# A prefix log-sum-exp kernel: one table set for Exp and Ln, and tiles of 512 rows instead of 256

## The chip, the cores and the metric

The kernel runs on one core of a Trainium2 chip. The metric is the device time of one execution in microseconds (us), lower is better. The unchanged kernel ("before") takes 1329.4 us as the median of three runs (1328.58 to 1329.96).

In the profiles PE is TensorE, which does the matrix products here (PEld is its loading of weights), ACT is ScalarE (Exp and Ln), DVE is VectorE (the adds), POOL is GpSimd and SP is SyncE; ACTq and SPq are the queues from which ScalarE and SyncE issue DMA transfers. L58 is line 58 of the kernel's file.

## The reference

The input `x` and the output are f32 arrays of shape (8, 4096, 2048). Along the second axis, each output row is the running log of the sum of exponentials:

```
out[:, 0] = x[:, 0]
for t in 1 .. 4095:
    mx        = max(out[:, t-1], x[:, t])
    out[:, t] = mx + log(exp(out[:, t-1] - mx) + exp(x[:, t] - mx))
```

The kernels here compute it as a running sum of `exp(x)` (matrix products with triangular matrices of ones, summed in PSUM) followed by a log. Both arrays must move: 268 MB in and 268 MB out.

## The kernel before

Two batch elements `j` are worked on in turn, so there are always two independent running sums. A tile holds 256 rows of one batch element: partition `p` holds rows `2p` and `2p+1` side by side, 4096 columns.

```python
    xpool = ... bufs=4        # input tiles,  f32,  16 KiB per partition each
    epool = ... bufs=4        # exp(x), bf16,        8 KiB
    opool = ... bufs=4        # output tiles, f32,  16 KiB
    ppool = ... bufs=1, PSUM  # two running sums [128, 2048] f32
    for bp in range(0, B, PAIR):
        ...
        for k in range(NBLK):
            for j in range(PAIR):
                ...
                xt = xpool.tile([P, 2 * D], f32)
                nc.sync.dma_start(out=xt, in_=x_v[b, k])            # L58, load, queue of SyncE
                et = epool.tile([P, 2 * D], bf16)
                nc.scalar.activation(et, xt, ACT.Exp)               # L61
                ...   # matmuls with Li and Ls: sum up to row 2p     # L65, L69
                ot = opool.tile([P, 2 * D], f32)
                nc.scalar.activation(ot[:, :D], ps, ACT.Ln)         # L75, first Ln
                nc.vector.tensor_add(ot[:, D:], ps, et[:, D:])      # L76, adds row 2p+1
                nc.scalar.activation(ot[:, D:], ot[:, D:], ACT.Ln)  # L77, second Ln
                nc.scalar.dma_start(out=o_v[b, k], in_=ot)          # L79, store, queue of ScalarE
                if k < NBLK - 1:
                    ...   # matmuls with Ui and Us complete the sum  # L84, L88
```

The program text does not fix the order of instructions on each engine. The framework that builds the kernel picks an order for each engine at build time, so that for example the Exp of the next tile goes ahead of the second Ln of this one.

The softmax here doesn't subtract the row's maximum and nothing guards it: scores larger than these inputs give would overflow.

Of the kernel before, what the change touches and what calls it, by code (L numbers as in the profile page):

```python
# [1 line left out]

# [4 lines left out]


@with_exitstack
def kernel(  # L10
    ctx: ExitStack,
    tc: tile.TileContext,
    x: bass.AP,
    out: bass.AP,
):
    nc = tc.nc
    f32 = mybir.dt.float32
    bf16 = mybir.dt.bfloat16
    ACT = mybir.ActivationFunctionType

    B, S, D = x.shape
    P = 128
    SB = 256
    NBLK = S // SB
    FD = 512
    NC = D // FD
    PAIR = 2

    const = ctx.enter_context(tc.tile_pool(name="const", bufs=1))
    Li = const.tile([P, P], bf16)  # L30
    masks.make_upper_triangular(nc, Li, val=1.0, diag=True)
    Ls = const.tile([P, P], bf16)
    masks.make_upper_triangular(nc, Ls, val=1.0, diag=False)
    Ui = const.tile([P, P], bf16)
    masks.make_lower_triangular(nc, Ui, val=1.0, diag=False)
    Us = const.tile([P, P], bf16)
    masks.make_lower_triangular(nc, Us, val=1.0, diag=True)

    xpool = ctx.enter_context(tc.tile_pool(name="xpool", bufs=4))
    epool = ctx.enter_context(tc.tile_pool(name="epool", bufs=4))  # L40
    opool = ctx.enter_context(tc.tile_pool(name="opool", bufs=4))
    ppool = ctx.enter_context(tc.tile_pool(name="ppool", bufs=1, space=bass.MemoryType.PSUM))

    x_v = x.rearrange("b (k p two) d -> b k p (two d)", p=P, two=2)
    o_v = out.rearrange("b (k p two) d -> b k p (two d)", p=P, two=2)

    for bp in range(0, B, PAIR):
        psums = [
            ppool.tile([P, D], f32, name=f"ps_{bp}_{j}", tag=f"ps{j}")
            for j in range(PAIR)  # L50
        ]
        for k in range(NBLK):
            for j in range(PAIR):
                b = bp + j
                ps = psums[j]

                xt = xpool.tile([P, 2 * D], f32)
                nc.sync.dma_start(out=xt, in_=x_v[b, k])  # L58

                et = epool.tile([P, 2 * D], bf16)  # L60
                nc.scalar.activation(et, xt, ACT.Exp)  # L61

                for c in range(NC):
                    lo, hi = c * FD, (c + 1) * FD
                    nc.tensor.matmul(  # L65
                        ps[:, lo:hi], Li, et[:, lo:hi],
                        start=(k == 0), stop=False, skip_group_check=True,
                    )
                    nc.tensor.matmul(  # L69
                        ps[:, lo:hi], Ls, et[:, D + lo : D + hi],  # L70
                        start=False, stop=False, skip_group_check=True,
                    )

                ot = opool.tile([P, 2 * D], f32)
                nc.scalar.activation(ot[:, :D], ps, ACT.Ln)  # L75
                nc.vector.tensor_add(ot[:, D:], ps, et[:, D:])  # L76
                nc.scalar.activation(ot[:, D:], ot[:, D:], ACT.Ln)  # L77

                nc.scalar.dma_start(out=o_v[b, k], in_=ot)  # L79

                if k < NBLK - 1:
                    for c in range(NC):
                        lo, hi = c * FD, (c + 1) * FD
                        nc.tensor.matmul(  # L84
                            ps[:, lo:hi], Ui, et[:, lo:hi],
                            start=False, stop=False, skip_group_check=True,
                        )
                        nc.tensor.matmul(  # L88
                            ps[:, lo:hi], Us, et[:, D + lo : D + hi],
                            start=False, stop=False, skip_group_check=True,  # L90
                        )


# [1 line left out]
_INS = ['x']  # L95
_OUTS = [((8, 4096, 2048), 'float32')]


# [23 lines left out]
```

## Time and profile before

| | before |
|---|---|
| time, median | 1329.4 us |
| ScalarE busy | 1268.8 us, 96% |
| of it table loads | 326 us, 254 loads |
| load queue and store queue, share of the 16 DMA engines | 51.4% + 47.3% |

These are lines of the profile's page of before: busy time per engine; the DMA's busy tenths and its GB/s in 40 slices of the span; the two DMA queues (packets, MB, share of the 16 engines' time; q1 is the loads, q10 the stores); the chain of waits by engine; and groups of instructions (count, busy us, mean ns, then the idle time before them).

```profile
PE 654.6 (49%) x1945; PEld 244.5 (18%) x1984; DVE 289.3 (22%) x128; ACT 1268.8 (96%) x638; POOL 1.9 (0%) x12
...
DMA  9999999999999999999999999999999999999976
GB/s 397 424 414 408 413 414 411 413 412 412 411 409 410 404 400 414 409 413 411 414 412 410 409 417 399 414 397 412 413 412 409 414 407 414 410 411 410 408 326 277
...
q1 hardware_dynamic: 18432, 268.44, 51.4%
q10 hardware_dynamic: 18432, 268.44, 47.3%
...
ACT 83%; PE 10%; issue 4%; ACTq 1%; DMA 1%; DVE 0%; another core or an unknown queue 0%; SPq 0%
...
L61 ACT ACTIVATE et<-xt 128x4096 bf16<-128x4096 f32 x128 | 462.9, 3617 | 9.1 <-DMA xt<-in_x_dram 7.7
...
L61 ACT ACT_TABLE_LOAD x127 | 162.9, 1283 | 3.1 <-PEq L106 0.8
L77 ACT ACT_TABLE_LOAD x84 | 107.8, 1283 | 1.5
...
L75 ACT ACT_TABLE_LOAD x43 | 55.2, 1283 | 0.7
```

ScalarE is the busy one, and a quarter of its work is table loads of 1283 ns, because Exp and Ln come from different table sets and alternate. The DMA is also shown at 9 tenths throughout.

Two views of waits say which of the two holds the other back. The first is ScalarE's waits, the second those of the load queue (what waited, on what; us in total, times, longest).

```profile
ACT et L61 <- DMA xt<-in_x_dram: 7.7, 2, 6.4
```

```profile
SPq L58 <- ACT et L61: 1207.2, 124, 11.9
```

ScalarE waited 7.7 us for loads in the whole run. The loads waited 1207 us for ScalarE to free an input buffer. ScalarE sets the pace.

The next view is four windows of 3 us of before, after start, end and length the busy time of each engine. The last three numbers of each line are TensorE's granted clock, the DMA's busy share and its GB/s.

```profile
609.00:612.00 3.00, 3.00 (x12) 1.17 (x10) 0.00 (x0) 2.98 (x2) 0.00 (x0) 0.71 1.02 437
612.00:615.00 3.00, 1.38 (x7) 0.52 (x6) 0.00 (x0) 2.99 (x3) 0.00 (x0) 1.00 0.97 371
615.00:618.00 3.00, 0.00 (x0) 0.00 (x0) 0.00 (x0) 2.53 (x2) 0.00 (x0) 0.92 1.07 339
618.00:621.00 3.00, 0.19 (x1) 0.10 (x1) 2.29 (x1) 2.97 (x3) 0.00 (x0) 0.50 0.89 360
```

Most of the time the DMA moves 431 to 437 GB/s. Once per three tiles it dips for some 9 us while its "busy" share stays near 1. In this dip (612 to 621 us) loads take 79% of the DMA's time, as the stores have nearly run out, and their packets get longer: 754 ns on average. The packet records have 611 ns as the usual time of a 16 KiB packet in both queues; 32768 of them on 16 engines make 1251 us. That is an estimate of the DMA's floor for this kernel.

### The profile page before, as it was taken

The page shows a single profiled execution, that of the slowest core. Times are in us where ns is not written, and L with a number is a line of the kernel's source. Part 1 is how long each engine was busy: PE and PEld are TensorE (multiplying, and loading weights), DVE is VectorE, ACT ScalarE, POOL GpSimd, SP SyncE. Part 2 cuts the span into 40 slices and gives each one's busy share as a digit, 9 for nine tenths or more (in the row PEclk, how much of TensorE's full clock was granted, in tenths as well). Part 3 has the DMA queues.
Part 4 walks back from the last instruction along what each step waited for, and adds up shares of the span by engine and source line. Part 5 has one row for each costly group of instructions (what it writes and reads, how often), then busy time and mean ns, then how long its engine had stood idle before and what let it go on. Part 6 is the DMA issues. An engine that isn't in the chain of part 4 may idle for free.

```text
span 1326.9 us, 5421 instructions
## 1 busy us (share of the span) xinstructions
PE 654.6 (49%) x1945; PEld 244.5 (18%) x1984; DVE 289.3 (22%) x128; ACT 1268.8 (96%) x638; POOL 1.9 (0%) x12
## 2 busy tenths in 40 slices
PE   4455544544454445544454555444544455555442
PEld 1111211211121111211111221111211121122110
DVE  1222222222222222222222222222222222222222
ACT  7999999999999999999999999999999999999996
POOL 0000000000000000000000000000000000000000
PEclk9777777777777777777677777777777777777776
DMA  9999999999999999999999999999999999999976
GB/s 397 424 414 408 413 414 411 413 412 412 411 409 410 404 400 414 409 413 411 414 412 410 409 417 399 414 397 412 413 412 409 414 407 414 410 411 410 408 326 277
DMA packets 36890, 537.22 MB, mean 405 GB/s; under 512 B 4096, under 2 KB 4096, under 8 KB 4096
## 3 DMA queue, kind: packets, MB, share of 16 engines
q1 hardware_dynamic: 18432, 268.44, 51.4%
q10 hardware_dynamic: 18432, 268.44, 47.3%
q8 instruction: 15, 0.25, 0.1%
q14 instruction: 11, 0.09, 0.0%
HBM read 268.44 MB, written 268.44 MB: 405 GB/s over the span
## 4 chain that ended last, share of the span: by engine, by line
ACT 83%; PE 10%; issue 4%; ACTq 1%; DMA 1%; DVE 0%; another core or an unknown queue 0%; SPq 0%
ACT et L61 35%; ACT ot L77 18%; ACT ot L75 12%; ACT L61 9%; ACT L77 8%; PE ps L65 6%; PE ps L69 4%; ACTq L79 1%; DMA xt<-in_x_dram 1%; ACT L75 0%; DVE ot L76 0%; ACTq L75 0%; SPq L58 0%
## 5 line engine op out<-in xcount | busy, mean ns | idle before, releaser
L76 DVE TENSOR_TENSOR ot<-ps,et 128x2048 f32<-128x2048 f32 x128 | 289.3, 2288 | 1025.7 <-ACT ot L75 1025.7
L61 ACT ACTIVATE et<-xt 128x4096 bf16<-128x4096 f32 x128 | 462.9, 3617 | 9.1 <-DMA xt<-in_x_dram 7.7
L84 PE MATMUL ps<-et,Ui 128*128 128x512 bf16 x480 | 261.3, 544 | 387.7 <-DVE ot L76 385.2
L65 PE MATMUL ps<-et,Li 128*128 128x512 bf16 x512 | 245.3, 479 | 268.4 <-ACT et L61 266.3
L75 ACT ACTIVATE ot<-ps 128x2048 f32<-128x2048 f32 x128 | 240.3, 1877 | 32.4 <-ACT ot L77 19.7
L88 PE MATMUL ps<-et,Us 128*128 128x512 bf16 x463 | 254.3, 549 | 0.0
L77 ACT ACTIVATE ot<-ot 128x2048 f32<-128x2048 f32 x128 | 239.8, 1904 | 1.6 <-DVE ot L76 0.6
L69 PE MATMUL ps<-et,Ls 128*128 128x512 bf16 x490 | 224.6, 458 | 0.0
L61 ACT ACT_TABLE_LOAD x127 | 162.9, 1283 | 3.1 <-PEq L106 0.8
L88 PEld LDWEIGHTS <-Us 128*128 128x128 bf16 x480 | 61.5, 128 | 499.3 <-issue 485.2
L69 PEld LDWEIGHTS <-Ls 128*128 128x128 bf16 x512 | 59.8, 117 | 360.8 <-issue 328.1
L77 ACT ACT_TABLE_LOAD x84 | 107.8, 1283 | 1.5
L84 PEld LDWEIGHTS <-Ui 128*128 128x128 bf16 x480 | 63.4, 132 | 107.9 <-issue 93.5
L65 PEld LDWEIGHTS <-Li 128*128 128x128 bf16 x512 | 59.8, 117 | 97.6 <-issue 60.6
L75 ACT ACT_TABLE_LOAD x43 | 55.2, 1283 | 0.7
masks.py:102 POOL TENSOR_SCALAR_AFFINE_SELECT Ui<-Ui 128x128 bf16<-128x128 bf16 x1 | 0.3, 299 | 0.0
masks.py:102 POOL TENSOR_SCALAR_AFFINE_SELECT Us<-Us 128x128 bf16<-128x128 bf16 x1 | 0.3, 298 | 0.0
masks.py:66 POOL TENSOR_SCALAR_AFFINE_SELECT Ls<-Ls 128x128 bf16<-128x128 bf16 x1 | 0.3, 297 | 0.0
masks.py:66 POOL TENSOR_SCALAR_AFFINE_SELECT Li<-Li 128x128 bf16<-128x128 bf16 x1 | 0.3, 296 | 0.0
masks.py:101 POOL MEMSET Ui<- 128x128 bf16 x1 | 0.2, 208 | 0.0
masks.py:101 POOL MEMSET Us<- 128x128 bf16 x1 | 0.2, 208 | 0.0
masks.py:65 POOL MEMSET Ls<- 128x128 bf16 x1 | 0.2, 206 | 0.0
(5 smaller groups left out, 0.6 us busy)
## 6 DMA issues: line engine op xcount, KB each, us to landing
xt<-in_x_dram SPq DMA_DIRECT2D x128, 2048.0 KB, 13.6
out_dram<-ot ACTq DMA_DIRECT2D x128, 2048.0 KB, 17.3
```

Source lines behind the costliest of these rows:

```text
L61: nc.scalar.activation(et, xt, ACT.Exp)
L65: nc.tensor.matmul(ps[:, lo:hi], Li, et[:, lo:hi], start=(k == 0), stop=False, skip_group_check=True,)
L69: nc.tensor.matmul(ps[:, lo:hi], Ls, et[:, D + lo : D + hi], start=False, stop=False, skip_group_check=True,)
L75: nc.scalar.activation(ot[:, :D], ps, ACT.Ln)
L76: nc.vector.tensor_add(ot[:, D:], ps, et[:, D:])
L77: nc.scalar.activation(ot[:, D:], ot[:, D:], ACT.Ln)
L79: nc.scalar.dma_start(out=o_v[b, k], in_=ot)
L84: nc.tensor.matmul(ps[:, lo:hi], Ui, et[:, lo:hi], start=False, stop=False, skip_group_check=True,)
L88: nc.tensor.matmul(ps[:, lo:hi], Us, et[:, D + lo : D + hi], start=False, stop=False, skip_group_check=True,)
```

## The change

The intent: load one table set that has both Exp and Ln, so that ScalarE no longer reloads tables; and put four rows in a partition, so that each descriptor moves 32 KiB. Rows two to four are made by chained adds on VectorE. The tile doubles to 4 MB, and so the buffers go from 4/4/4 to 3/2/2 (input/bf16/output) to fit: 192 KiB per partition.

```diff
+    nc.scalar.preload_act_table_set("natural_log_exp_and_others")
-    SB = 256
-    NBLK = S // SB
+    R = 4
+    NBLK = S // (P * R)
...
-    xpool ... bufs=4    epool ... bufs=4    opool ... bufs=4
+    xpool ... bufs=3    epool ... bufs=2    opool ... bufs=2
...   (matmuls moved to a helper, the same number of them)
-                xt = xpool.tile([P, 2 * D], f32)
+                xt = xpool.tile([P, R * D], f32)
                 nc.sync.dma_start(out=xt, in_=x_v[b, k])
-                nc.scalar.activation(et, xt, ACT.Exp)
+                nc.scalar.activation(et[:, :half], xt[:, :half], ACT.Exp)      # L80
+                nc.scalar.activation(et[:, half:], xt[:, half:], ACT.Exp)      # L81
...
-                nc.vector.tensor_add(ot[:, D:], ps, et[:, D:])
+                nc.scalar.activation(ot[:, :D], ps, ACT.Ln)                     # L86
+                nc.vector.tensor_add(ot[:, D : 2 * D], ps, et[:, D : 2 * D])    # L87
+                for r in range(2, R):
+                    nc.vector.tensor_add(                                       # L89
+                        ot[:, r * D : (r + 1) * D],
+                        ot[:, (r - 1) * D : r * D],
+                        et[:, r * D : (r + 1) * D],
+                    )
                 nc.scalar.activation(ot[:, D:], ot[:, D:], ACT.Ln)              # L95
                 nc.scalar.dma_start(out=o_v[b, k], in_=ot)                      # L97
```

(The first Ln, L86, was there before too; it is shown for its line number.)

More of the change, by code (lines that the diff above doesn't have):

```diff
@@ L37, with accumulate @@
     masks.make_lower_triangular(nc, Us, val=1.0, diag=True)
-    xpool = ctx.enter_context(tc.tile_pool(name="xpool", bufs=4))
-    epool = ctx.enter_context(tc.tile_pool(name="epool", bufs=4))
-    opool = ctx.enter_context(tc.tile_pool(name="opool", bufs=4))
+    xpool = ctx.enter_context(tc.tile_pool(name="xpool", bufs=3))
+    epool = ctx.enter_context(tc.tile_pool(name="epool", bufs=2))
+    opool = ctx.enter_context(tc.tile_pool(name="opool", bufs=2))
     ppool = ctx.enter_context(tc.tile_pool(name="ppool", bufs=1, space=bass.MemoryType.PSUM))
-    x_v = x.rearrange("b (k p two) d -> b k p (two d)", p=P, two=2)
-    o_v = out.rearrange("b (k p two) d -> b k p (two d)", p=P, two=2)
+    x_v = x.rearrange("b (k p r) d -> b k p (r d)", p=P, r=R)
+    o_v = out.rearrange("b (k p r) d -> b k p (r d)", p=P, r=R)
+    def accumulate(ps, et, first, rest, start):
+        for r in range(R):
+            w = first if r == 0 else rest
+            for c in range(NC):
+                lo, hi = c * FD, (c + 1) * FD
+                nc.tensor.matmul(
+                    ps[:, lo:hi], w, et[:, r * D + lo : r * D + hi],
+                    start=(start and r == 0), stop=False, skip_group_check=True,
+                )
     for bp in range(0, B, PAIR):
@@ L55 @@
                 ps = psums[j]
-                xt = xpool.tile([P, 2 * D], f32)
+                xt = xpool.tile([P, R * D], f32)
                 nc.sync.dma_start(out=xt, in_=x_v[b, k])
-                et = epool.tile([P, 2 * D], bf16)
-                nc.scalar.activation(et, xt, ACT.Exp)
-                for c in range(NC):
-                    lo, hi = c * FD, (c + 1) * FD
-                    nc.tensor.matmul(
-                        ps[:, lo:hi], Li, et[:, lo:hi],
-                        start=(k == 0), stop=False, skip_group_check=True,
-                    )
-                    nc.tensor.matmul(
-                        ps[:, lo:hi], Ls, et[:, D + lo : D + hi],
-                        start=False, stop=False, skip_group_check=True,
-                    )
-                ot = opool.tile([P, 2 * D], f32)
-                nc.scalar.activation(ot[:, :D], ps, ACT.Ln)
-                nc.vector.tensor_add(ot[:, D:], ps, et[:, D:])
+                et = epool.tile([P, R * D], bf16)
+                half = R * D // 2
+                nc.scalar.activation(et[:, :half], xt[:, :half], ACT.Exp)
+                nc.scalar.activation(et[:, half:], xt[:, half:], ACT.Exp)
+                accumulate(ps, et, Li, Ls, k == 0)
+                ot = opool.tile([P, R * D], f32)
+                nc.scalar.activation(ot[:, :D], ps, ACT.Ln)
[5 more added lines that the diff above has]
+                        et[:, r * D : (r + 1) * D],
+                    )
                 nc.scalar.activation(ot[:, D:], ot[:, D:], ACT.Ln)
@@ L81 @@
                 if k < NBLK - 1:
-                    for c in range(NC):
-                        lo, hi = c * FD, (c + 1) * FD
-                        nc.tensor.matmul(
-                            ps[:, lo:hi], Ui, et[:, lo:hi],
-                            start=False, stop=False, skip_group_check=True,
-                        )
-                        nc.tensor.matmul(
-                            ps[:, lo:hi], Us, et[:, D + lo : D + hi],
-                            start=False, stop=False, skip_group_check=True,
-                        )
+                    accumulate(ps, et, Ui, Us, False)
 _INS = ['x']
```

## The prediction

> **What bounds it now.** ScalarE. The page's busy line has ACT at 1268.8 of 1326.9 us (96%); the waits view shows ScalarE waiting only 7.7 us for loads, while the load queue waits 1207 us for ScalarE to free its input buffers. The chain of waits is 83% ACT. Of ACT's time 326 us (162.9 + 107.8 + 55.2 in the groups, 254 loads of 1283 ns) is table loading, because Exp and Ln alternate. Without it ACT would need 943 us.
>
> But DMA stands right behind: the slices show 9 tenths and about 411 GB/s. Stretches of 3 us (600 to 693 us) read 431 to 437 GB/s mostly, with one dip per 30.7 us (three tiles) to about 340 to 390 GB/s over 9 us, when the stores have run out and a nearly empty load queue shows long packets. The page's queue lines give 0.473 x 1327 x 16 / 16384 = 613 ns per 16 KiB store packet, 666 ns per load packet; the packet records have 611 ns as the usual value for both. 32768 packets of 611 ns on 16 engines are 1251 us. I read the rest (about 55 us of lengthened load packets) as ScalarE not asking early enough, not as a DMA limit. The Trainium skill ("DMA: Bandwidth & Descriptors", "Where 436 GB/s comes from") puts the fabric ceiling at 435 GB/s; 431 to 437 agrees. So the change can win 5 to 6%, not the 25% of the table loads.
>
> **What the change does.**
> - Table loads: 254 to 1 or 2. The Trainium skill ("ScalarE: Activation LUTs", "Table sets") lists Exp and Ln in this set. Saves 325 us of ACT.
> - ACT per 512-row tile: two Exp of 3.62, Ln of 2048 at 1.88, Ln of 6144 at about 5.33 (estimate from the slope between the 1.90 and 3.62 us activations): 14.4 us, times 64 is 925 us, about 73%.
> - VectorE: 192 adds of about 2.29 us, 440 us (from 289), chained.
> - Matmuls: same number.
> - DMA: same bytes, half the packets. 4-byte packets take 9 ns; if that is the fixed part, a 32 KiB packet takes 1213 ns and the floor is 1242 us (estimate).
> - Buffers: 3/2/2 of double size. An output buffer's loop (Ln 1.9 + adds 6.9 + Ln 5.3 + about 2 + store 19.6 at half rate = 36 us) is under two tile periods (39 us): tight, but while stores are out, loads run at full rate.
>
> **Sum.** First packet after about 2.6 us; DMA 1242 to 1251; tail with DMA idle about 18 (last load: Exp 7.2, matmuls 3.4, Ln and adds 8.8, Ln 5.3, issue, then a 9.8 us store; one other store fills part); remaining dips about 5; the time sits 2.5 above the span. I say **1274 us, range 1258 to 1300**. Faster by over 2%: 0.87; within 2%: 0.11; slower: 0.02.
>
> **What the profile would show.** ACT at 70 to 75% with one table load; ScalarE waiting hundreds of us for loads; slices at 425 to 435 GB/s throughout; 8192 data packets per queue at 1213 to 1225 ns; DVE 440 us; the chain no longer mostly ACT.
>
> **What would make it wrong.** (1) The dips belong to the DMA, so it stays at 411 GB/s: near 1325. (2) Two output or two bf16 buffers make ScalarE wait for stores or matmuls while the input buffers stand full, so DMA idles each tile: 1300 or more. (3) Table loads stay; even 190 leave ACT at 1170, under DMA. (4) Ramp and tail grow with the doubled tile by more than 10 us.

## The result, and the profile after

The changed kernel takes 1396.7 us (median of four runs, 1396.3 to 1398.33), against 1329.7 us for before in the same comparison. The ratio is 1.051 (95% interval 1.049 to 1.052): 5% slower, where 4% faster was predicted. Ratios in this document are the mean time of one kernel's fast runs over that of the other's in the same rounds, so not quite the ratio of the medians that are quoted. Results are correct unless said otherwise.

The lines of the changed kernel's page that answer to those of before:

```profile
PE 579.5 (42%) x1882; PEld 220.5 (16%) x1920; DVE 434.1 (31%) x192; ACT 905.5 (65%) x257; POOL 1.9 (0%) x12
...
DMA  9989989899898989989899797997979989899865
GB/s 406 420 348 406 435 340 427 363 421 407 368 427 363 406 376 406 435 361 423 376 416 430 316 430 335 414 434 313 430 336 406 436 335 429 351 407 434 337 266 241
...
q10 hardware_dynamic: 9216, 268.44, 45.7%
q1 hardware_dynamic: 9216, 268.44, 45.5%
...
ACT 35%; DMA 28%; DVE 26%; issue 10%; ACTq 0%; PE 0%
...
L95 ACT ACTIVATE ot<-ot 128x6144 f32<-128x6144 f32 x64 | 338.9, 5318 | 308.2 <-DVE ot L89 308.2
...
L89 DVE TENSOR_TENSOR ot<-ot,et 128x2048 f32<-128x2048 f32 x128 | 288.9, 2288 | 2.2
...
L27 ACT ACT_TABLE_LOAD x1 | 1.3, 1283 | 0.8 <-PEq L115 0.8
```

What was predicted of the parts happened: one table load, ScalarE busy for 905 us (925 predicted), VectorE for 434 us, 8192 data packets in each queue. What was predicted of the whole did not: ScalarE does not wait hundreds of us for loads, and the slices do not stay at 425 to 435 GB/s. The DMA is no longer always busy. Its queues add up to 91.2% of the span instead of 98.7%, so packets fill all but 8.8% of 1394.6 us, about 123 us, and the slices, but for the last two, swing between 313 and 436 GB/s. The chain of waits is now split three ways, ScalarE 35%, DMA 28%, VectorE 26%: no engine is full, they wait for one another in turn.

ScalarE's waits of the changed kernel:

```profile
ACT ot L95 <- DVE ot L89: 308.2, 47, 9.1
ACT ot L86 <- DMA out_dram<-ot: 143.3, 15, 14.7
ACT et L80 <- DMA xt<-in_x_dram: 10.9, 1, 10.9
```

It hardly waits for loads (10.9 us). It waits 308 us for VectorE's adds (47 times) and 143 us for stores, 15 times, some 9.6 us each: the first Ln (L86) needs an output buffer that is still being stored. Busy 905.5, adds 308 and stores 143 make 1357 of the 1394.6 us.

Here is one such wait. First ScalarE, then VectorE, of the changed kernel in order of time (start, duration, engine, line, operation, tile; in brackets the idle time before it and what ended it).

```profile
660.59 3.60 ACT L81 ACTIVATE et<-xt 128x4096 bf16<-128x4096 f32 x1
664.09 1.85 ACT L86 ACTIVATE ot<-ps 128x2048 f32<-128x2048 f32 x1
673.38 1.88 ACT L86 ACTIVATE ot<-ps 128x2048 f32<-128x2048 f32 x1 [7.43 <-DMA out_dram<-ot]
684.21 10.54 ACT L95 ACTIVATE ot<-ot 128x6144 f32<-128x6144 f32 x2 [8.96 <-DVE ot L89]
689.57 5.55 ACTq L97 DMA_DIRECT2D out_dram<-ot  x2
```

```profile
665.98 2.29 DVE L87 TENSOR_TENSOR ot<-ps,et 128x2048 f32<-128x2048 f32 x1 [21.17 <-ACT ot L86]
675.29 2.29 DVE L87 TENSOR_TENSOR ot<-ps,et 128x2048 f32<-128x2048 f32 x1 [7.02 <-ACT ot L86]
677.49 8.89 DVE L89 TENSOR_TENSOR ot<-ot,et 128x2048 f32<-128x2048 f32 x4
```

Tile one gets its first Ln at 664.09 and its first add at 665.98. But the lists of both engines then name tile two: ScalarE's next instruction is tile two's first Ln, which waits until 673.38 for an output buffer; VectorE's next is tile two's first add, which waits for that Ln. Tile one's remaining adds stand behind it, in a row of four with tile two's, and its second Ln starts at 684.21. So tile one's 4 MB store is issued 25.5 us after its first Ln, although its own work is 1.9 + 6.9 + 5.3 = 14.1 us. In the two windows of 3 us before that issue the DMA runs dry (the last two numbers are its busy share and GB/s):

```profile
684.00:687.00 3.00, 0.00 (x0) 0.00 (x0) 2.38 (x2) 2.79 (x1) 0.00 (x0) 0.50 0.41 175
687.00:690.00 3.00, 0.00 (x0) 0.00 (x0) 0.00 (x0) 3.00 (x2) 0.00 (x0) 0.50 0.00 0
```

The three input buffers are full, and no store is there yet.

The Trainium skill ("PSUM — Partial Sum Buffer", section "Engine vs sequencer instructions") says that the queues of ScalarE and VectorE are strict FIFO. The two timelines agree: nothing passes the waiting instruction, although tile one's second add could have started some 9 us earlier, at the end of its first (668.27).

### The profile page after: what moved, and what is told of

The parts are those of the page before. It is cut to its first block, busy times and chain, and to the rows that moved or that the text cites. A ratio compares the mean times of both kernels' runs of the same rounds, so it can differ in the third digit from the quotient of the medians.

```text
span 1394.6 us, 4663 instructions
## 1 busy us (share of the span) xinstructions
PE 579.5 (42%) x1882; PEld 220.5 (16%) x1920; DVE 434.1 (31%) x192; ACT 905.5 (65%) x257; POOL 1.9 (0%) x12
## 4 chain that ended last, share of the span: by engine, by line
ACT 35%; DMA 28%; DVE 26%; issue 10%; ACTq 0%; PE 0%
DMA out_dram<-ot 27%; ACT ot L95 20%; DVE ot L89 18%; DVE ot L87 8%; ACT ot L86 6%; ACT et L80 6%; ACT et L81 3%; DMA xt<-in_x_dram 1%; PE ps L60 0%; ACTq L97 0%; ACTq L86 0%; ACTq L80 0%
## 5 line engine op out<-in xcount | busy, mean ns | idle before, releaser
L95 ACT ACTIVATE ot<-ot 128x6144 f32<-128x6144 f32 x64 | 338.9, 5318 | 308.2 <-DVE ot L89 308.2
L87 DVE TENSOR_TENSOR ot<-ps,et 128x2048 f32<-128x2048 f32 x64 | 146.6, 2292 | 933.4 <-ACT ot L86 933.4
L89 DVE TENSOR_TENSOR ot<-ot,et 128x2048 f32<-128x2048 f32 x128 | 288.9, 2288 | 2.2
L60 PE MATMUL ps<-et,Li 128*128 128x512 bf16 x251 | 91.3, 499 | 468.0 <-ACT et L80 467.7
L80 ACT ACTIVATE et<-xt 128x4096 bf16<-128x4096 f32 x64 | 230.6, 3604 | 18.1 <-DMA xt<-in_x_dram 10.9
L81 ACT ACTIVATE et<-xt 128x4096 bf16<-128x4096 f32 x64 | 230.4, 3601 | 0.0
L86 ACT ACTIVATE ot<-ps 128x2048 f32<-128x2048 f32 x64 | 119.1, 1861 | 145.6 <-DMA out_dram<-ot 143.3
L60 PE MATMUL ps<-et,Us 128*128 128x512 bf16 x658 | 204.2, 471 | 1.5 <-issue 1.1
L60 PE MATMUL ps<-et,Ui 128*128 128x512 bf16 x220 | 83.7, 517 | 278.5 <-DVE ot L87 278.0
L60 PEld LDWEIGHTS <-Ls 128*128 128x128 bf16 x768 | 86.3, 112 | 166.1 <-issue 108.9
L60 PEld LDWEIGHTS <-Li 128*128 128x128 bf16 x256 | 28.3, 111 | 517.5 <-issue 493.0
L60 PEld LDWEIGHTS <-Ui 128*128 128x128 bf16 x224 | 25.1, 112 | 323.0 <-issue 310.3
L27 ACT ACT_TABLE_LOAD x1 | 1.3, 1283 | 0.8 <-PEq L115 0.8
```

The lines of the kernel that those rows point to most:

```text
L27: nc.scalar.preload_act_table_set("natural_log_exp_and_others")
L60: nc.tensor.matmul(ps[:, lo:hi], w, et[:, r * D + lo : r * D + hi], start=(start and r == 0), stop=False, skip_group_check=True,)
L80: nc.scalar.activation(et[:, :half], xt[:, :half], ACT.Exp)
L81: nc.scalar.activation(et[:, half:], xt[:, half:], ACT.Exp)
L87: nc.vector.tensor_add(ot[:, D : 2 * D], ps, et[:, D : 2 * D])
L89: nc.vector.tensor_add(ot[:, r * D : (r + 1) * D], ot[:, (r - 1) * D : r * D], et[:, r * D : (r + 1) * D],)
```

## The experiments

Eighteen more kernels ran. The table has ScalarE's account for those that the argument rests on, all from the busy lines and the waits views, in us. "Adds" is the second Ln waiting for VectorE, "stores" the first Ln waiting for an output buffer, "matmuls" the first Ln waiting for PE. 3/2/2 and the like are numbers of input, bf16 and output buffers; "8 columns" and "64 columns" are the changed kernel with a needless Exp of so many columns, which changes the order (see below). Times are medians; the waits are those of the one profiled run.

| kernel | time | busy | adds | stores | loads | matmuls |
|---|---|---|---|---|---|---|
| before | 1329 | 1269 | 1 | 0 | 8 | 11 |
| changed | 1397 | 906 | 308 | 143 | 11 | 2 |
| 256 rows, combined tables | 1260 | 916 | 1 | 289 | 8 | 31 |
| 256 rows, 3/2/2 | 1353 | 921 | 10 | 198 | 8 | 219 |
| 256 rows, 3/2/4 | 1314 | 921 | 11 | 0 | 8 | 354 |
| changed, with table loads | 1358 | 1034 | 270 | 15 | 11 | 1 |
| changed, 2/2/3 | 1294 | 907 | 309 | 0 | 43 | 10 |
| changed, later loads | 1322 | 906 | 308 | 69 | 11 | 2 |
| changed, Ln per row | 1418 | 923 | 166 | 297 | 11 | 2 |
| 8 columns | 1311 | 914 | 153 | 194 | 13 | 2 |
| 64 columns | 1290 | 917 | 336 | 0 | 14 | 0 |

### The combined table set alone

```diff
     ACT = mybir.ActivationFunctionType
+    nc.scalar.preload_act_table_set("natural_log_exp_and_others")     # in the kernel before
```

> The kernel before with the combined table set alone (256-row tiles, 4/4/4 buffers). Theory (the DMA limit of the prediction was right, and the slowdown comes from the 512-row tile with few buffers): the loads of tables go from 254 to 1, DMA stays supplied, about 1272 to 1285 us, 430 GB/s in the slices. Rival (the 411 GB/s of before was already the limit of mixed loads and stores): 1315 to 1330 us, with ACT idle.

Measured: 1259.5 us (1259.0 to 1259.64), ratio 0.948 (0.946 to 0.949). This is the fastest correct kernel, 5% faster than before, and below even the theory's range. Lines of its page:

```profile
PE 648.3 (52%) x1984; PEld 238.8 (19%) x1984; DVE 293.1 (23%) x128; ACT 916.2 (73%) x385; POOL 1.9 (0%) x12
...
DMA  9999999999999999999999999999999999999997
GB/s 385 431 432 430 431 431 431 430 431 431 429 431 431 431 429 432 431 431 431 431 432 430 430 432 431 429 432 431 431 430 430 432 429 433 430 431 430 431 431 325
...
q1 hardware_dynamic: 18432, 268.44, 50.0%
q10 hardware_dynamic: 18432, 268.44, 49.9%
```

The DMA runs at 429 to 433 GB/s in every slice between the first and the last, and its queues take 99.9% of the span. So the dips of before were ScalarE's doing, and the DMA floor of the prediction (1251 us) was right. Summed over both queues and shared over 16 engines, the packets' excess over 611 ns fell from about 56 us to under 3. ScalarE's 289 us of waits for stores cost nothing here: both queues always hold work, and the wait is for the DMA, which is the limit.

This splits the change in two: the table set is worth -70 us, so the 512-row tile with its buffers costs +137 us on top of it. (The two parts are not independent, as the run with table loads below shows.)

### 256 rows with as few buffers

```diff
-    xpool bufs=4, epool bufs=4, opool bufs=4      # combined tables, 256 rows
+    xpool bufs=3, epool bufs=2, opool bufs=2
```

> The kernel before with the combined table set and 3 input, 2 bf16 and 2 output buffers, as the changed kernel has, but of half the size. Theory (the number of output buffers alone starves the DMA, whatever the tile size): 1360 us or more, with ScalarE waiting for stores and fully idle DMA in every tile. Rival (it is the longer serial chain of the four-row tile, Ln, three adds, Ln, before a 4 MB store): below 1310 us.

Measured: 1353.2 us (1346.6 to 1365.2), ratio 1.016 (1.011 to 1.021). Neither number was hit by the median, but the rival is out: with half-size tiles fewer buffers eat the gain of the tables, and more. (With fewer buffers the build also chose another order on ScalarE than with 4/4/4, so the count and the order that came with it are not separated.) Two waits appear in the profiled run, the slowest of the four at 1365 us: 198 us for stores and 219 us for matmuls, so it is not output buffers only.

```diff
+    xpool bufs=3, epool bufs=2, opool bufs=4      # the order on ScalarE's list is the same as with 3/2/2
```

> 256-row tiles, combined tables, 3 input, 2 bf16 and 4 output buffers; its ScalarE order is the same as that of the run with 3/2/2 (1353 us). Theory (output buffers are what starves it): 1265 to 1290 us, no waits for stores to speak of. Rival (two bf16 buffers or three input buffers cost as much; 219 us of waits for matmuls point there): 1310 us or more.

Measured: 1314.4 us (1314.0 to 1314.9), ratio 0.989 (0.987 to 0.990), outside the theory's range and in the rival's. Two more output buffers took the 198 us of waits for stores away and brought 39 us; waits for matmuls grew to 354 us. In this build ScalarE runs first Ln, Exp, second Ln of one tile at a time, and each first Ln waits some 3 us for matmuls. Which of the other two pools causes that was not tried. So at 256 rows theory and rival each explain a part: output buffers cost about 39 us, and the other 55 us (1314 against 1260) come with the other two pools and the order that the build chose for them.

### The changed kernel with table loads

```diff
-    nc.scalar.preload_act_table_set("natural_log_exp_and_others")
```

> The changed kernel without the combined table set, so table loads return. Theory (in the changed kernel the chain Ln, adds, Ln, store, buffer is the limit and ScalarE is on it part of the time): table loads of 1.28 us that fall on the chain lengthen it, 1400 to 1480 us. Rival (ScalarE has 35% of slack, so table loads vanish in it): within 1% of 1397 us.

Measured: 1358.4 us (two runs, 1357.0 and 1359.7), ratio 1.022 (1.020 to 1.024). Both expectations missed: with 128 us more work for ScalarE the changed kernel is 38 us faster. Leaving the table loads aside, the lists of ScalarE and VectorE are the same instruction for instruction, so this is not another order. ScalarE's waits for stores fell from 143 to 15 us. So the table set, worth 70 us with 256 rows, costs 38 us here, and with table loads in both kernels the 512-row tile costs only 29 us (1358 against 1329). A possible reason: the table loads delay the Exp, so the input buffers come free later and the next loads start later. The next run tests that.

### Loads that start later

```diff
+    hold = const.tile([P, 1], f32)
...
                 nc.scalar.activation(ot[:, :D], ps, ACT.Ln)
+                nc.gpsimd.tensor_add(hold, xt[:, :1], ot[:, :1])   # keeps xt until here
```

> The changed kernel, where GpSimd reads one column of the input tile after the first Ln of that tile, so that an input buffer comes free (and the next 4 MB load starts) some 5 to 15 us later; ScalarE's order is unchanged. Found so far: the four-row kernel with table loads (same order on ScalarE) takes 1358 us, without them 1397 us. Theory (a faster ScalarE frees input buffers earlier, and the loads then share the DMA with the stores that the output buffers wait for): later loads make the stores land sooner, ScalarE's 143 us of waits for stores shrink, the time falls to 1350 to 1385 us. Rival (fewer loads in flight only leave DMA more idle; the table loads helped for another reason): 1400 us or more.

Measured: 1322.4 us (1321.1 to 1326.8), ratio 0.995 (0.993 to 0.997): 74 us faster than the changed kernel, for one needless instruction on GpSimd per tile. It is better than the theory's range. ScalarE's waits (L97 is the second Ln here, L87 the first):

```profile
ACT ot L97 <- DVE ot L91: 308.1, 47, 9.0
ACT ot L87 <- DMA out_dram<-ot: 68.8, 15, 9.3
```

Waits for adds are the same 308 us; waits for stores fell by 74.5 us, which is the whole gain. Loads and stores run on the same 16 DMA engines. The Trainium skill ("DMA: Bandwidth & Descriptors", "Issuing engines are not separate DMA queues") says that DMAs interleave there whichever engine issued them, and the packet records of the changed kernel agree: while both queues have work, loads take 52% of the engines and stores 48%. In the changed kernel an input buffer comes free early, its load takes half of the DMA from a store that ScalarE is waiting for, and then the loads run out of buffers and the DMA idles. Starting the load later lets the store go first. The traces bear this out: the 15 stores that ScalarE waited for took 25.2 us on average from issue to its next Ln in the changed kernel, with loads on 42% of the DMA meanwhile; here they took 20.2 us, with loads on 33%. And the queues now fill 97.3% of the span (48.9 + 48.4) instead of 91.2%, so the time in which the DMA is free fell from 123 to 36 us.

### One buffer moved from input to output

```diff
-    xpool bufs=3, epool bufs=2, opool bufs=2
+    xpool bufs=2, epool bufs=2, opool bufs=3
```

> The changed kernel with one 32 KiB buffer moved from the input pool to the output pool (2/2/3 instead of 3/2/2). The order of the instructions on ScalarE is nearly the same. Theory (two output buffers are the cause): ScalarE's 143 us of waits for stores go and the time falls to about 1320 to 1360 us, though loads have less room. Rival (any loss of room for loads costs as much, the total of buffers is what matters): 1390 us or more.

Measured: 1293.7 us (1290.4 to 1294.8), ratio 0.973 (0.971 to 0.975): 103 us faster than the changed kernel with the same memory, again better than the range. ScalarE's list is the same, so the comparison is clean. Its waits:

```profile
ACT ot L95 <- DVE ot L89: 309.2, 47, 9.1
ACT et L80 <- DMA xt<-in_x_dram: 43.3, 12, 11.0
```

No wait for stores is left; 32 us more are spent waiting for loads.

### The output tile in halves, and a Ln for each row

The first of these stores each half of the output tile by itself, from two pools of half tiles, after its own Ln.

```diff
-                ot = opool.tile([P, R * D], f32)
+                oa = opool.tile([P, 2 * D], f32, tag="oa")    # rows one and two
+                ob = opool.tile([P, 2 * D], f32, tag="ob")    # rows three and four
...
+                nc.scalar.activation(oa[:, D:], oa[:, D:], ACT.Ln)
+                nc.scalar.dma_start(out=o_v[b, k][:, : 2 * D], in_=oa)
+                nc.scalar.activation(ob, ob, ACT.Ln)
+                nc.scalar.dma_start(out=o_v[b, k][:, 2 * D :], in_=ob)
```

> The changed kernel with each output tile in two halves of 16 KiB per partition (2 buffers each, the same memory), each with its own Ln and its own 2 MB store, the first half stored while rows three and four are still to be done. Theory (two whole output tiles, each held from the first Ln to the landing of a 4 MB store, are the bottleneck): halves come free sooner and the DMA has a store to move earlier, 1270 to 1330 us. Rival (total bytes of output buffer count, not their grain): 1380 us or more.

Measured: 1296.9 us (1291.3 to 1302.8), ratio 0.975 (0.971 to 0.979), as the theory said: 100 us faster in the same memory. Waits for stores are 11 us. The build's order changed here as well, but not to fewer pairs in which both first Ln come in a row: there are 24 of 32 (16 in the changed kernel). How much of the gain is the halves and how much the order is not separated.

```diff
-                nc.scalar.activation(ot[:, D:], ot[:, D:], ACT.Ln)
+                for r in range(1, R):
+                    nc.scalar.activation(ot[:, r*D:(r+1)*D], ot[:, r*D:(r+1)*D], ACT.Ln)
```

> The changed kernel with the Ln over 6144 columns cut into three of 2048, so that a row's Ln runs beside the add of the next row; one 4 MB store as before. Theory (the serial chain Ln, three adds, Ln of 5.3 us, store holds the output buffer): some 3.5 us shorter per tile where nothing else waits, up to 64 x 3.5 / 2 = 110 us in all, so 1290 to 1370 us. Rival (only the store's time matters): within 1% of 1397 us.

Measured: 1417.7 us (1416.4 and 1418.9), ratio 1.066 (1.064 to 1.068). A miss: slower, though the wait for adds halved to 166 us. The build's order had changed too. Both tiles' first Ln now come ahead of any second Ln in every pair (in the changed kernel, in every second pair), with five single-row Ln ahead of the first store. Waits for stores doubled: 297 us, 31 times. This pointed to the order.

The two ideas that worked, together: halves of the output tile with 2 input and 3 + 3 half output buffers.

> 512-row tiles, combined tables, output tiles in halves, 2 input, 2 bf16 and 3 + 3 half output buffers. Theory (output space was the limit, input space is then next): 1265 to 1295 us, ScalarE waiting for loads instead of stores. If it beats the 1259.5 us of the combined tables alone, the larger descriptors (1213 ns for 32 KiB against 2 x 611 ns) were worth having.

Measured: 1268.9 us (1267.7 to 1270.3), ratio 0.954 (0.953 to 0.956), the best correct kernel with 512 rows; but ScalarE still waits for adds, not for loads as expected, and it doesn't beat the 1259.5 us of the tables alone.

### Two adds taken away

```diff
-   (adds of rows three and four)
+                nc.scalar.activation(ot[:, 2 * D :], et[:, 2 * D :], ACT.Ln)      # wrong on purpose
```

> Wrong result on purpose: the changed kernel without the adds of rows three and four; their Ln reads the bf16 tile directly. Order on ScalarE differs. Theory (the chained adds of VectorE, 4.6 us per tile, are part of the chain that holds an output buffer): 1280 to 1350 us with two output buffers all the same. Rival (VectorE has slack, 31% busy, so its adds cost nothing): within 1% of 1397 us.

Measured: 1267.6 us (1267.0 and 1268.3), ratio 0.953 (0.951 to 0.955), with a wrong result, as intended. VectorE was busy only 31% in the changed kernel, yet without two of its three adds the kernel is 129 us faster, and ScalarE's wait for adds is 2 us: better than the theory's range, and the adds stand in the chain. How much of the gain is the adds and how much the new order that came with the edit, this run doesn't tell.

### The order of the two tiles

A needless Exp of a few columns ahead of the real ones makes the build choose other orders, with next to no work. The first try was long, 1296 columns.

```diff
+                nc.scalar.activation(et[:, :pad], xt[:, :pad], ACT.Exp)    # pad = 1296, 64 or 8
                 nc.scalar.activation(et[:, :half], xt[:, :half], ACT.Exp)
```

> The changed kernel with a needless Exp of 1296 columns (about 1.27 us) ahead of each tile's first Exp: 81 us more work for ScalarE, same result. The build then also puts ScalarE's instructions in another order: never the first Ln of two tiles in a row ahead of the second Ln of either, as the changed kernel has it in every second pair. Theory (ScalarE runs in order, so the first Ln of tile two, waiting for an output buffer, keeps back the second Ln and the store of tile one; and earlier freed input buffers start loads against the stores): clearly faster in spite of more work, 1290 to 1360 us, waits for stores under 70 us. Rival (neither matters, work on ScalarE is cheap or costs): 1397 us or more.

Measured: 1347.0 us (1346.8 to 1347.1), ratio 1.013 (1.012 to 1.015): as the theory said, 50 us faster with 77 us more work (982.5 against 905.5 us busy), and no wait for stores at all.

> The same with 64 columns, 56 more, 3 us of ScalarE in all. The build then never puts the two first Ln ahead of the second Ln of the first tile (the order of the run with 1296 columns, 1347 us). Theory of order: 1290 to 1345 us, hardly any wait for stores. Rival (the needless work itself helped by freeing input buffers later): within 1% of the run with 8 columns.

Measured: 1289.8 us (1289.4 to 1294.8), ratio 0.971 (0.969 to 0.973): 107 us faster than the changed kernel, with its tile size, adds and buffers, and a needless 0.24 us instruction per tile. Its whole list on ScalarE differs from the changed kernel's, the Exp of tile two's second half coming before that of its first half, too. Its order is that of the 1296-column run, so the 57 us between the two are what 1232 more columns (66 us of ScalarE's busy time) cost in this order. ScalarE and VectorE of this run, to be laid beside the timelines of the changed kernel (L88 first Ln, L97 second Ln, L89 and L91 the adds):

```profile
657.15 1.85 ACT L88 ACTIVATE ot<-ps 128x2048 f32<-128x2048 f32 x1
658.91 3.60 ACT L82 ACTIVATE et<-xt 128x4096 bf16<-128x4096 f32 x1
666.02 5.32 ACT L97 ACTIVATE ot<-ot 128x6144 f32<-128x6144 f32 x1 [3.51 <-DVE ot L91]
671.25 1.86 ACT L88 ACTIVATE ot<-ps 128x2048 f32<-128x2048 f32 x1
671.37 0.34 ACTq L99 DMA_DIRECT2D out_dram<-ot  x1
680.12 5.32 ACT L97 ACTIVATE ot<-ot 128x6144 f32<-128x6144 f32 x1 [7.01 <-DVE ot L91]
```

```profile
659.04 2.29 DVE L89 TENSOR_TENSOR ot<-ps,et 128x2048 f32<-128x2048 f32 x1 [18.34 <-ACT ot L88]
661.37 4.62 DVE L91 TENSOR_TENSOR ot<-ot,et 128x2048 f32<-128x2048 f32 x2
673.14 2.29 DVE L89 TENSOR_TENSOR ot<-ps,et 128x2048 f32<-128x2048 f32 x1 [7.16 <-ACT ot L88]
675.47 4.62 DVE L91 TENSOR_TENSOR ot<-ot,et 128x2048 f32<-128x2048 f32 x2
```

Tile one's three adds now follow each other (659.04 to 665.99), its second Ln starts at 666.02, and only then comes tile two's first Ln, which finds a buffer free; tile one's store is issued at 671.37. The mean time from the first Ln to the issue of the tile's store, over all 64 tiles of the trace, is 14.2 us here and 19.2 us in the changed kernel. Its one large wait:

```profile
ACT ot L97 <- DVE ot L91: 336.4, 64, 7.0
```

Busy 917 plus 336 us for adds make 1253 of 1288 us. In this order, ScalarE's work and its waits for VectorE make up nearly the whole time.

> The changed kernel with a needless Exp of 8 columns per tile. The build then puts the first Ln of both tiles ahead of the second Ln of either in every pair (the changed kernel does so in every second pair). Theory (in-order ScalarE: tile two's first Ln, waiting for an output buffer, holds back tile one's second Ln and store): 1405 to 1440 us, some 30 waits for stores, 250 us or more in all. Rival (order does not matter): 1397 to 1405 us.

Measured: 1310.6 us (1303.6 to 1314.6), ratio 0.985 (0.982 to 0.989). With both first Ln ahead in every pair this was to be slower than the changed kernel; it is 86 us faster. Against 64 columns it is 21 us slower, with 194 us of waits for stores where that has none, so the direction between these two is as expected. But the order of first Ln on ScalarE is not the whole story. VectorE's list differs as well: here one add of rows three and four goes ahead of tile two's first add; in the changed kernel's bad pair none does.

```diff
-                nc.scalar.activation(et[:, :half], xt[:, :half], ACT.Exp)
                 nc.scalar.activation(et[:, half:], xt[:, half:], ACT.Exp)
+                nc.scalar.activation(et[:, :half], xt[:, :half], ACT.Exp)      # swapped, nothing added
```

> The changed kernel with its two Exp lines swapped (second half first), nothing added. The build then orders ScalarE and VectorE as in the run with 8 columns: one add of rows three and four goes ahead of tile two's first add, instead of none in every second pair. Theory (the order is what matters, not the needless Exp): 1295 to 1320 us. Rival (the needless Exp matters): within 1% of 1397 us.

Measured: 1317.2 us (1311.8 to 1320.0), ratio 0.990 (0.988 to 0.993). Swapping two lines that do the same work takes 79 us off the changed kernel. It has the orders of the 8-column kernel and about its time, so the needless Exp is not what helped. The swap also changes which half is ready first (the list of the 8-column kernel has the second half first, too), and that part is not separated from the order.

### Do later loads and more output buffers help in the other orders?

Four runs repeat the two cures in the two new orders, with the lists of ScalarE and VectorE unchanged.

> The run with 64 columns, and the input buffer held until the first Ln of its tile, as in the run that went from 1397 to 1322 us. Theory (loads against stores only cost where ScalarE waits for a store): nothing to win here, within 1.5% of the run with 64 columns, or slower. Rival (the DMA itself runs better with fewer loads in flight): again 3 to 5% faster.

Measured: 1289.7 us (1289.5 to 1289.8), ratio 0.970 (0.969 to 0.972).

> The run with 64 columns with 2/2/3 buffers and the same order on ScalarE. Theory (with the better order two output buffers suffice, as no first Ln waits for a store): within 1.5% of the run with 64 columns. Rival (two output buffers are the limit in any order): 2% or more faster, towards 1265 to 1290 us.

Measured: 1289.9 us (1289.7 to 1290.2), ratio 0.970 (0.969 to 0.972). Both are within 0.2 us of the median with 64 columns alone, and both wait 336.3 us for adds. Where no first Ln waits for a store, neither cure has anything to give, and two output buffers are enough.

> The run with 8 columns with 2/2/3 buffers, same order. Theory (in this order a third output buffer takes the waits for stores away, as it did in the changed kernel): waits for stores under 20 us, 1265 to 1295 us. Rival (two input buffers starve the loads instead): 1305 us or more.

Measured: 1276.1 us (1272.1 to 1277.2), ratio 0.960 (0.959 to 0.962): the waits for stores (194 us) are gone, as expected. Waits for matmuls (85 us) and loads (71 us) take part of their place. This is also 14 us faster than the 64-column order with either set of buffers (1290 us), so with three output buffers the order with both first Ln in a row is the faster one.

> The run with 8 columns (first Ln of both tiles ahead in every pair, 1310.6 us, 194 us of waits for stores), with the input buffer held until the first Ln of its tile; same order on ScalarE and VectorE. Theory (later loads leave the DMA to the store that ScalarE waits for): waits for stores below 130 us, 1280 to 1303 us. Rival (nothing to gain, or the loads now come too late): 1305 us or more.

Measured: 1315.7 us (1313.2 to 1320.0), ratio 0.990 (0.988 to 0.992). A miss: waits for stores stay at 192 us and the time with them. So later loads help in the changed kernel's order and not in this one. The queue lines say a part of why: in the 8-column order the two queues already fill 96.8% of the span (97.0% with later loads), where the changed kernel had 91.2%, so there was little idling of the DMA to remove. Why its waits for stores did not shrink was not found.

## Why the prediction was wrong, point by point

- **The limits of before: right.** ScalarE set the pace, the DMA stood behind at 1251 us, and the dips were ScalarE's. The table set alone gave 1259.5 us, near the low end of the range that was given for the whole change.
- **The costs of the parts: right.** One table load; ScalarE's groups at 919 us (230.6 + 230.4 + 119.1 + 338.9) against 925; adds of 2.29 us, 434 us in all against 440 (instructions overlap a little, so ScalarE's busy time is 905.5 and not 919); the usual 32 KiB packet at 1213 ns, as estimated from the 9 ns of 4-byte packets.
- **The step that failed** is the line on buffers: an output buffer's loop of "Ln 1.9 + adds 6.9 + Ln 5.3 + about 2 + store 19.6" = 36 us, "under two tile periods (39 us): tight, but while stores are out, loads run at full rate". It summed a tile's own work as if no other tile stood between and as if every store took 19.6 us. Two terms failed. First, the measured time from first Ln to store issue is 19.2 us instead of 14.1, since both engines' in-order lists put tile two's first Ln and first add, waiting for a buffer, ahead of tile one's adds. Second, the store: from issue to the last packet's end it took 18.5 us on average, which is near the 19.6, but the 15 stores that ScalarE waited for took 25.2 us until its next Ln. The period per tile became 21.3 us (from the first store's issue to the last's, over 63), not 19.5. The 64-column order puts the 14.1 right (14.2 measured) and takes 107 us off; a third output buffer, with the order unchanged, takes 103 us off.
- **"While stores are out, loads run at full rate"** (read as: while there is no store to move) held only as long as an input buffer was free, and that was not reckoned: input buffers that come free early start loads that share the DMA with the awaited store, and then are full when the DMA has nothing else to do (0 GB/s from 687 to 690 us). Delaying the loads was worth 74 us in the changed kernel, all of it out of the waits for stores.
- **ScalarE's slack was no slack.** At 65% busy it looked free; but in the changed kernel it waits 308 us for the chained adds in between, and 336 us in the 64-column order. There busy plus adds is 1253 us, on top of which come the start and the end of the run: 1290 us, where the DMA would allow 1242 to 1251.
- Of the reasons named for being wrong, number (2) is the one that came: output buffers, and waits for stores while input buffers stand full. All the outcomes that were not faster by over 2% had a chance of 0.13 together. The larger wait, 308 us for VectorE's adds, is in none of the reasons. The danger was named and the sum that dismissed it was too simple.

Open are two things: why later loads do not shorten the waits for stores in the 8-column order, and how much of the gap between the changed kernel and the 8-column kernel is VectorE's list and how much the swapped halves.

## What to carry to other kernels

When an engine that set the pace gets faster, ask who then holds each buffer, for how long, and in which order the in-order engines will serve the two tiles in flight: a buffer's loop is not the sum of its own instructions if the next tile's waiting instruction stands between them. Doubling a tile halves the number of buffers, and here packets of 1213 instead of 2 x 611 ns (0.7%) could not pay for that. Try the cheap part of a change alone: one line, the table set, gave 70 us, and the rest of the change took 137 us back. And read the time in which the DMA is free beside the sum of one engine's waits: here 289 us of waits for stores cost nothing where the queues filled 99.9% of the span, and 143 us cost much where they filled 91.2%.

## What the Trainium skill lacked or had wrong

- "ScalarE: Activation LUTs", "What ACT_TABLE_LOAD costs", gives 1283 ns for the load and about 1380 ns for a drain with every switch. The load is 1283 ns here, but no such drain shows: in before, a Ln ends at 606.14, the load starts at 606.15 and the Exp at 607.45, so a switch costs about 1.3 us.
- "DMA: Bandwidth & Descriptors", "Rules for kernel authors", asks for 1 MiB or more per DMA for bandwidth; that section says nothing about what larger transfers cost in buffers, and no page was found with a figure for it. Going from 2 MB to 4 MB per transfer saved 0.7% per byte and, with 3/2/2 buffers and the order that the build chose, cost 137 us.
- "HBM Reference", "Specifications (TRN2)", has about 425 GB/s for a core that streams alone; loads and stores together held 429 to 433 GB/s in the slices of the combined-tables kernel between the first and the last, 1 to 2% more.
- No page that was read says that loads and stores of one core should be timed against each other: starting loads later made the changed kernel 74 us faster (and gained nothing in two other orders).
